# A hybrid RWKV-7 and neighbourhood-attention layer: low halves of four w_out weights made by ACT and adding DMAs, the first sums into x ahead of a small transpose, and two steps of the load order moved

## The chip, the cores and the metric

One core of one Trainium2 chip runs the kernel. The core has five instruction engines, each with an order of its own: TensorE (PE), VectorE (DVE), ScalarE (ACT), GpSimd (POOL) and SyncE (SP), which here only issues DMAs. POOL issues some DMAs too. The metric is the device time of one execution in microseconds (us).

## What is computed

One layer over 640 tokens: 512 noisy latent tokens on a grid 64 wide and 128 context tokens. The layer, shortened from the reference (the shifts sh, scales sc and gates g come from a conditioning vector; the recurrent and the attention branch are two functions of their own, not shown):

```python
sh1, sc1, g1, sh2, sc2, g2 = _modulation(cvec, p["w_ada"], p["b_ada"])
h = _rmsnorm(x, p["norm1_g"]) * (1.0 + sc1) + sh1
u_rw, u_na, gate_rw, gate_na = jnp.split(h @ p["w_in"], IN_SPLITS, axis=-1)
o_rw, s_new = _rwkv_branch(u_rw, s0, ...)                 # 512 wide
o_na = _na_latent(q, k, v, ctx_k, ctx_v, p["na_rpb"])     # 512 wide
merged = (jax.nn.sigmoid(gate_rw) * (o_rw @ p["w_o_rwkv"])
          + jax.nn.sigmoid(gate_na) * (o_na @ p["w_o_na"]))   # 1024 wide
x = x + g1 * (merged @ p["w_out"])                        # w_out: 1024 x 1024
h2 = _rmsnorm(x, p["norm2_g"]) * (1.0 + sc2) + sh2
x = x + g2 * ((jax.nn.silu(h2 @ p["ffn_w1"]) * (h2 @ p["ffn_w3"])) @ p["ffn_w2"])
```

All of it is float32 in and out.

## The kernel before, in words

Each matmul is made of three on fp32r operands: high half of the weight by high and by low half of the activation, and low half of the weight by high half of the activation. A weight tile of 128x1024 (512 KB) goes through three steps. `wdma` (L156 to L168) has SP load it into a staging tile `wst`. `wcast` (from L179) makes the high half `whi` with a rounding copy on ACT (L185) and the low half `wlo`, as a rule by a subtraction on DVE (L188, `wst` less `whi`). With `eng=pool` the low half comes another way: ACT writes the rounded weight negated into `wlo` (L183) and a DMA issued by POOL adds `wst` onto it (L184). `wload` does both steps.

In the middle part, `stream` (from L788) runs a fixed list of weight units one after the other and feeds their matmuls in between other work. It keeps the staging loads of two units ahead queued on SP, and queues them at the start of a unit. The units a0 to a3 and b0 to b3 are the merge: they multiply w_o by the attention and recurrent outputs `o`, seven tiles that come back from memory (`o_d`) by `o_load` (L1473): tiles 0 to 3 for the a units, 4 and 5, and 6 when it is there, for the b units. The second part is loaded before unit a0 runs. What the units add up is kept in `mt` and other tiles of 128x640. The eighth tile of the outputs, `o3`, never leaves the core and is merged last.

The last merge, `last_gen` (L1638 to L1656), runs 16 halves of 320 tokens, two for each of eight feature tiles. For a half PE runs 3 matmuls (L1649) into one of three PSUM buffers `fl`; DVE multiplies by the gate's tile `pre` or `tr` (L1650), which frees that buffer, and adds what the units left in `mt` (L1652); ACT makes the high half of m (L1653) and POOL the low half (L1654). From the sixth half on, PE puts two matmuls of w_out's first half (L303) behind each half; PE's order is written out there by hand, the other engines' order comes from a scheduler.

w_out's first half (`w0`) takes four weights, w_out[0] to w_out[3], as chunks of two feature tiles each; 30 matmuls a chunk, 120 in all, into accumulators `acc` for five blocks of 128 tokens. Chunks 0 to 2 run over all blocks, and the last (chunk 3) block by block, so that block 0 is ready first. w_out[0] is cast before the merge. Then `x` (L1678) and the gate rows `G` (L1683) are loaded; 16 small PE transposes (L1709) bring shift and scale rows into `pc`, from which DVE makes s and m (L1711 to L1713); and `add_gated` (L1685 to L1689) does for each block `tt = acc * G` (L1688), which frees the accumulator, and `x = x + tt` (L1689). The second half, with w_out[4] to w_out[7], follows, and behind it the feed-forward part (L1810 and on, with L1854 for its low halves) to the end.

Staging tiles and high and low halves come from pools: two staging tiles and two pairs of halves in the pool of the outer part (w_out[0], [4], [6]), two of each in a pool for w_out[1] to [3], and one staging tile and two pairs in a pool that opens when that one closes (w_out[5], [7]).

Of the kernel before, what the change touches and what calls it, by code (L numbers as in the profile page):

```python
# [107 lines left out]
def body(ctx: ExitStack, tc: tile.TileContext, xs, xp, cols, consts, w_ada, b_row, w_rw, w_qkv,  # L108
# [26 lines left out]
    def nm(s):  # L135
        cn[0] += 1
        return f"{s}_{cn[0]}"
# [59 lines left out]
    def wload(src, eng=None):  # L197
        return wcast(wdma(src), eng)
# [81 lines left out]
    def tok_gen(pss, pp, lhs_hl, chunks, kts, toks, tag="acc", bufs=5, tail=1, keep=None):  # L280
# [7 lines left out]
        for ci, src in enumerate(chunks):  # L288
            ws.append(src if isinstance(src, (tuple, list)) else wload(src))
# [494 lines left out]
    def stream(order):  # L784
# [10 lines left out]
        for i, g in enumerate(order):  # L795
            while len(ds) < min(i + 3, len(us)):
                ds.append(us[len(ds)][1]())
# [5 lines left out]
            for j in range(n):  # L803
                if j == n // 8:
                    later(lambda i=i: cast(i + 1), (1.05, 0), -off[0])
                next(it)
                tick(1)
                if j == n - 1:
                    drain(it)
                    done.add(g)  # L810
                    if i + 1 < len(order) and order[i + 1] == "a0":
                        o_load(4, 6)
                        if "O2" in marks:
                            o_load(6, 7)
                yield True
# [261 lines left out]
    with ExitStack() as s3:  # L1077
# [394 lines left out]

        def o_load(a, b):  # L1473
# [3 lines left out]
            for q in range(a, b):  # L1477
# [100 lines left out]
        with tc.manual_schedule(engines=FIRST):  # L1578
# [54 lines left out]
            c0 = wload(w_out[0])  # L1633
# [30 lines left out]
    w0 = w_out_gen(pss, [c0] + [w_out[q] for q in range(1, 4)], range(5))  # L1664
# [39 lines left out]
    pc = pp.tile([P, 512], F32, tag="tp", name=nm("pc"))  # L1704
    for j in range(2):
        arow = sb.tile([P, 1024], F32, tag="xn", bufs=3, name=nm("arow"))[0:2, :]
        sp.dma_start(arow, adr[:, (6 + 2 * j) * 512:(8 + 2 * j) * 512])
        for kt in range(8):
            pe.transpose(pc[:, 16 * j + 2 * kt:16 * j + 2 * kt + 2], arow[:, kt * 128:(kt + 1) * 128],  # L1709
                         K[0:2, KO["ident"]:KO["ident"] + 2])  # L1710
    dve.tensor_copy(s2, V(pc[:, :], [[2, 8], [1, 2]]))  # L1711
    dve.tensor_scalar(out=m2, in0=V(pc[:, :], [[2, 8], [1, 2]], 16), scalar1=1.0, scalar2=None, op0=ALU.add)
    dve.tensor_tensor(out=m2, in0=m2, in1=V(C[:, :], [[1, 8], [0, 2]], CO["n2"]), op=ALU.mult)  # L1713
    for i in range(5):
        add_gated(pss[i], i, 0, 0.5)
# [375 lines left out]
```

## Time and profile before

| what | us |
|---|---|
| median of 3 runs (lowest, highest) | 1175.58 (1175.09, 1177.53) |
| the profiled execution, its own time | 1175.43 |
| its span in the trace | 1173.7 |
| PE busy in the span | 1125.1 |
| DVE busy | 778.6 |
| ACT busy | 531.9 |
| POOL busy | 193.2 |

The mean granted clock of PE in the profiled execution was 0.991 of full speed. All times below are in us from the start of the span. A row of a timeline gives start, duration, engine, line, operation, result<-operands, shapes and the number of instructions in the group, and in brackets the idle time ahead of it with what ended that. Rows named SPq or POOLq are issues of DMAs. A wait view gives, for an engine, the total, the number and the longest of its waits by line and by what it waited for. The whole span has three stretches for what follows: the middle part to 662, the last merge with w_out's first half from 662 to 704, and the second half and the feed-forward part after that.

### The profile page before, as it was taken

What the parts mean: (1) busy time and instruction counts of PE and PEld (TensorE: products, weight loads), DVE (VectorE), ACT (ScalarE), POOL (GpSimd) and SP (SyncE); (2) the same over time, 40 slices, a digit from 0 to 9 for tenths busy, and PEclk for the clock granted to TensorE, in tenths of its full rate; (3) what the DMA queues carried; (4) which work ended last, traced back from release to release, by engine and by line L of the source; (5) the groups of instructions that cost most, each with busy time, mean ns of one, the idle gap of its engine ahead of it and who ended that gap; (6) DMA issues with size and microseconds to landing.
All of it is one profiled execution on the core that took longest, in us unless ns stands there. A gap on an engine that the chain in (4) does not pass through costs nothing.

```text
span 1173.7 us, 26876 instructions
## 1 busy us (share of the span) xinstructions
PE 1125.1 (96%) x11160; PEld 995.6 (85%) x11160; DVE 778.6 (66%) x1643; ACT 531.9 (45%) x1050; POOL 193.2 (16%) x260
## 2 busy tenths in 40 slices
PE   6999999999999999999899899999999999999998
PEld 4688877789888988888788777899899989998997
DVE  4565465559558747935576847887577756875775
ACT  4444666554564665556443324654224423441330
POOL 1162244320101202111100231100000000001000
PEclk9999999999999999999899999999999999999999
DMA  9752767554433523433843641312312222232122
GB/s 338 265 115 83 240 227 231 188 162 103 105 84 93 139 69 91 111 99 93 281 122 114 216 159 55 108 58 88 108 54 91 91 89 65 80 108 90 54 81 99
DMA packets 60194, 148.11 MB, mean 126 GB/s; under 512 B 7428, under 2 KB 22404, under 8 KB 60072
## 3 DMA queue, kind: packets, MB, share of 16 engines
q1 hardware_dynamic: 55464, 131.56, 34.3%
q0 software_dynamic: 3744, 13.63, 6.0%
q8 instruction: 88, 1.44, 0.5%
q10 hardware_dynamic: 864, 1.20, 0.4%
q14 instruction: 34, 0.28, 0.1%
HBM read 118.41 MB, written 14.32 MB: 113 GB/s over the span
## 4 chain that ended last, share of the span: by engine, by line
PE 60%; DVE 10%; ACT 3%; issue 2%; DMA 2%; SPq 0%; POOL 0%; DVEq 0%; ACTq 0%; POOLq 0%
PE f L1810 21%; PE acc L303 16%; PE fl L216 11%; PE w L1367 1%; PE w L1394 1%; DVE pr L1293 1%; PE w L1407 1%; PE mm L216 1%; PE w L1379 1%; PE w L1191 1%; DVE RL L1297 1%; DVE Rt L1327 1%; PE w L1424 1%; PE w L1385 1%; PE w L1239 1%
## 5 line engine op out<-in xcount | busy, mean ns | idle before, releaser
L1810 PE MATMUL f<-t,whi 128*128 128x320 f32 x640 | 142.4, 311 | 0.0
L1810 PE MATMUL f<-b,whi 128*128 128x320 f32 x608 | 135.6, 310 | 2.1 <-ACT b L204 1.8
L303 PE MATMUL acc<-whi,u 128*128 128x512 f32 (+1 forms) x448 | 136.0, 385 | 0.0
L216 PE MATMUL fl<-h,whi 128*128 128x320 f32 x672 | 121.2, 320 | 1.0 <-issue 1.0
L1810 PEld LDWEIGHTS f<-t,whi 128*128 128x128 f32 x640 | 108.1, 189 | 0.0
L185 ACT CAST whi<-wst 128x1024 fp32r<-128x1024 f32 (+1 forms) x77 | 79.1, 1033 | 62.3 <-PE acc L303 42.7
L216 PEld LDWEIGHTS fl<-h,whi 128*128 128x128 f32 x672 | 101.3, 188 | 5.8 <-issue 1.2
L1810 PEld LDWEIGHTS f<-b,whi 128*128 128x128 f32 x608 | 102.0, 188 | 3.3 <-ACT b L204 2.2
L1810 PE MATMUL f<-t,wlo 128*128 128x320 f32 x320 | 99.4, 310 | 0.0
L303 PEld LDWEIGHTS acc<-whi,u 128*128 128x128 f32 x448 | 83.5, 188 | 16.7
L1810 PE MATMUL f<-b,wlo 128*128 128x320 f32 x304 | 94.3, 310 | 2.2 <-DVE wlo L1854 2.2
L1851 ACT CAST whi<-ws 128x1024 fp32r<-128x1024 f32 x40 | 42.0, 1051 | 109.0 <-PE f L1810 44.4
L188 DVE TENSOR_TENSOR wlo<-wst,whi 128x1024 fp32r<-128x1024 f32 (+2 forms) x59 | 63.4, 1086 | 36.9 <-ACT whi L185 36.3
L303 PE MATMUL acc<-wlo,u 128*128 128x512 f32 (+1 forms) x224 | 86.3, 385 | 0.0
L1865 POOL TENSOR_TENSOR ws<-wst 128x512 f32<-128x512 f32 x20 | 28.0, 1402 | 340.8 <-DVE wlo L1854 226.7
L303 PE MATMUL acc<-whi,h 128*128 128x512 f32 x240 | 78.0, 399 | 0.9 <-DVE h L428 0.9
L216 PE MATMUL fl<-h,wlo 128*128 128x320 f32 x336 | 63.3, 321 | 0.0
L1688 DVE SCALAR_TENSOR_TENSOR tt<-acc,G 128x512 f32<-128x512 f32 (+1 forms) x51 | 34.5, 680 | 42.7 <-PE acc L303 42.7
L1851 ACT CAST whi<-wst 128x1024 fp32r<-128x1024 f32 (+1 forms) x48 | 41.3, 869 | 42.3 <-PE acc L303 25.1
L1810 PEld LDWEIGHTS f<-t,wlo 128*128 128x128 f32 x320 | 60.5, 189 | 0.0
L1810 PEld LDWEIGHTS f<-b,wlo 128*128 128x128 f32 x304 | 57.2, 188 | 2.5 <-DVE wlo L1854 2.5
L1854 DVE TENSOR_TENSOR wlo<-ws,whi 128x1024 fp32r<-128x1024 f32 x40 | 54.7, 1366 | 6.6 <-ACT whi L1851 6.6
(342 smaller groups left out, 2507.8 us busy)
## 6 DMA issues: line engine op xcount, KB each, us to landing
wst<-in_w_dram SPq DMA_DIRECT2D x66, 512.0 KB
wst<-in_w_rw_dram SPq DMA_DIRECT2D x31, 512.0 KB
wlo<-wst POOLq DMA_DIRECT2D x26, 512.0 KB, 4.8
wa<-in_w_ada_dram SPq DMA_DIRECT2D x24, 512.0 KB
f<-in_w_ada_dram SPq DMA_DIRECT2D x16, 512.0 KB
wst<-in_w_qkv_dram SPq DMA_DIRECT2D x12, 512.0 KB
o<-o_d SPq DMA_DIRECT2D x14, 320.0 KB
x<-in_xs_dram SPq DMA_DIRECT2D x8, 512.0 KB
```

Source lines behind the costliest of these rows:

```text
L185: act.copy(hi[:, :n], st[:, :n])
L188: dve.tensor_tensor(out=lo[:, a:b], in0=st[:, a:b], in1=hi[:, a:b].bitcast(F32), op=ALU.subtract)
L216: pe.matmul(ps[:, :t1 - t0], w[:, a:a + 128], x[:, k0 + kt, t0:t1], start=n == 0, stop=n == 3 * nk - 1)
L303: pe.matmul(pss[i][:, a:b], lhs(x, kt, ts_), w[:, cs_], start=ki == 0 and n == 0, stop=ki == last and n == 2)
L1191: pe.matmul(pr[h][hrows[h ^ i], o_], x[hrows[h], :], R_[hrows[h], l, :], start=True, stop=True)
L1239: pe.matmul(pt[h][hrows[h ^ i], o_], S.BK[l // 10][hrows[h], l % 10, i, :], idh(h), start=True, stop=True)
L1293: dve.tensor_tensor(out=prv, in0=V(RL[:, s + 1 + a, :], [[32, b - a], [0, s]], s), in1=V(RL[:, s, :], [[0, b - a], [1, s]]), op=ALU.mult)
L1688: dve.scalar_tensor_tensor(out=tt, in0=ps[:, a:b], scalar=c, in1=G[:, g, sl], op0=ALU.mult, op1=ALU.mult)
L1810: pe.matmul(ps[:, :H2], w_[:, c_], x_[:, kt, :], start=first and kt + n == 0, stop=last and kt == 3 and n == 2, skip_group_check=more)
L1851: act.copy(r[0][:, :width], src())
L1854: dve.tensor_tensor(out=r[1][:, :width], in0=src(), in1=r[0][:, :width].bitcast(F32), op=ALU.subtract)
L1865: eng_x(PRM["se"][i - 1]).tensor_tensor(out=o_, in0=x, in1=y, op=op)
```

## The change

There are four edits. First, `stream` queues the staging loads of the unit after next in the middle of a unit (a quarter in for some sizes) and no longer at its start. Second, `o_load(4, 6)` is called when a0 has run, not before it; `got` keeps a tile from being loaded twice. Third, w_out[0] to w_out[3] get `eng=pool`. Fourth, the sums into x come ahead of the transposes in the program, in a region in which DVE keeps the order in which the code is written.

```diff
--- before.py
+++ after.py
@@ -277,7 +277,7 @@
             pass
         return pss
 
-    def tok_gen(pss, pp, lhs_hl, chunks, kts, toks, tag="acc", bufs=5, tail=1, keep=None):
+    def tok_gen(pss, pp, lhs_hl, chunks, kts, toks, tag="acc", bufs=5, tail=1, keep=None, eng=None):
 
 
         pss.update((i, pp.tile([P, 512], F32, tag="tp" if i == 5 else tag, bufs=3 if i == 5 else bufs,
@@ -286,7 +286,7 @@
         last = len(kts) - 1
         ws, n0 = [] if keep is None else keep, len(chunks) - tail
         for ci, src in enumerate(chunks):
-            ws.append(src if isinstance(src, (tuple, list)) else wload(src))
+            ws.append(src if isinstance(src, (tuple, list)) else wload(src, eng))
             ks = [2 * ci + k for k in range(2)]
 
             if ci >= n0:
@@ -793,8 +793,6 @@
         ds.append(us[1][1]())
         yield True
         for i, g in enumerate(order):
-            while len(ds) < min(i + 3, len(us)):
-                ds.append(us[len(ds)][1]())
             while wait.get(g) not in marks:
                 yield False
             n, f = us[i][0], us[i][3]
@@ -803,12 +801,14 @@
             for j in range(n):
                 if j == n // 8:
                     later(lambda i=i: cast(i + 1), (1.05, 0), -off[0])
+                if j == (n // 2 if n == 48 else n // 4) and i + 2 < len(us):
+                    ds.append(us[i + 2][1]())
                 next(it)
                 tick(1)
                 if j == n - 1:
                     drain(it)
                     done.add(g)
-                    if i + 1 < len(order) and order[i + 1] == "a0":
+                    if g == "a0":
                         o_load(4, 6)
                         if "O2" in marks:
                             o_load(6, 7)
@@ -1470,11 +1470,14 @@
                 marks.add("O2")
 
 
+        got = set()
+
         def o_load(a, b):
 
             if not o:
                 o.extend(Two([]) for _ in range(2))
-            for q in range(a, b):
+            for q in sorted(set(range(a, b)) - got):
+                got.add(q)
                 for i, (t, t_d) in enumerate(zip(o, o_d)):
                     if len(t.ts) == q // 4:
                         t.ts.append(hp_t("o", i, q // 4))
@@ -1630,7 +1633,7 @@
                 S = S2
             weave(og)
             need(*(f"b{i}" for i in range(4)))
-            c0 = wload(w_out[0])
+            c0 = wload(w_out[0], pool)
 
 
     pp = open_pool(ctx, "pp4", bufs=3, space=PSUM)
@@ -1661,7 +1664,7 @@
     pss = {}
     trp = open_pool(hs, "trp")
     weights(hs, 2, 2)
-    w0 = w_out_gen(pss, [c0] + [w_out[q] for q in range(1, 4)], range(5))
+    w0 = w_out_gen(pss, [c0] + [w_out[q] for q in range(1, 4)], range(5), eng=pool)
     with tc.manual_schedule(engines=MANUAL):
         for h, _ in enumerate(last_gen()):
             for _ in range(PRM["lw"][h]):
@@ -1701,18 +1704,19 @@
                       name=f"b{x[0]}{x[1]}{i}") for i in range(2)] for x in halves2}
     sb = open_pool(ctx, "p4")
     load_gate(4)
-    pc = pp.tile([P, 512], F32, tag="tp", name=nm("pc"))
-    for j in range(2):
-        arow = sb.tile([P, 1024], F32, tag="xn", bufs=3, name=nm("arow"))[0:2, :]
-        sp.dma_start(arow, adr[:, (6 + 2 * j) * 512:(8 + 2 * j) * 512])
-        for kt in range(8):
-            pe.transpose(pc[:, 16 * j + 2 * kt:16 * j + 2 * kt + 2], arow[:, kt * 128:(kt + 1) * 128],
-                         K[0:2, KO["ident"]:KO["ident"] + 2])
-    dve.tensor_copy(s2, V(pc[:, :], [[2, 8], [1, 2]]))
-    dve.tensor_scalar(out=m2, in0=V(pc[:, :], [[2, 8], [1, 2]], 16), scalar1=1.0, scalar2=None, op0=ALU.add)
-    dve.tensor_tensor(out=m2, in0=m2, in1=V(C[:, :], [[1, 8], [0, 2]], CO["n2"]), op=ALU.mult)
-    for i in range(5):
-        add_gated(pss[i], i, 0, 0.5)
+    with tc.manual_schedule(engines={mybir.EngineType.DVE}):
+        for i in range(5):
+            add_gated(pss[i], i, 0, 0.5)
+        pc = pp.tile([P, 512], F32, tag="tp", name=nm("pc"))
+        for j in range(2):
+            arow = sb.tile([P, 1024], F32, tag="xn", bufs=3, name=nm("arow"))[0:2, :]
+            sp.dma_start(arow, adr[:, (6 + 2 * j) * 512:(8 + 2 * j) * 512])
+            for kt in range(8):
+                pe.transpose(pc[:, 16 * j + 2 * kt:16 * j + 2 * kt + 2], arow[:, kt * 128:(kt + 1) * 128],
+                             K[0:2, KO["ident"]:KO["ident"] + 2])
+        dve.tensor_copy(s2, V(pc[:, :], [[2, 8], [1, 2]]))
+        dve.tensor_scalar(out=m2, in0=V(pc[:, :], [[2, 8], [1, 2]], 16), scalar1=1.0, scalar2=None, op0=ALU.add)
+        dve.tensor_tensor(out=m2, in0=m2, in1=V(C[:, :], [[1, 8], [0, 2]], CO["n2"]), op=ALU.mult)
 
 
     nr = [{} for _ in range(5)]
```

The changed file has three more lines ahead of the last merge, so L1650 before is L1653 behind, and L1688 is L1691.

Where the third edit shows on DVE, the rows at the start of the last merge are as follows, before and behind. wlo_9058 is the low half of w_out[0], wlo_9457 and wlo_9464 are that of w_out[4], the rows of L1525 and L1528 belong to the last unit b3, and pre is the gate of the first feature tile.

```order
L1525 SCALAR_TENSOR_TENSOR mx_9017<-mx_9017,fl_9041 128x320
L1527 TENSOR_TENSOR bv_8415<-bv_8415,mx_9017 128x320
L188 TENSOR_TENSOR wlo_9058<-wst_9055,whi_9057 128x1024
L188 TENSOR_TENSOR wlo_9457<-wst_9454,whi_9456 128x1024
L1650 SCALAR_TENSOR_TENSOR pre_9079<-pre_9079,fl_9095 128x320
L1650 SCALAR_TENSOR_TENSOR pre_9079<-pre_9079,fl_9103 128x320
```

```order
L1528 SCALAR_TENSOR_TENSOR mx_9017<-mx_9017,fl_9041 128x320
L1530 TENSOR_TENSOR bv_8415<-bv_8415,mx_9017 128x320
L188 TENSOR_TENSOR wlo_9464<-wst_9461,whi_9463 128x1024
L1653 SCALAR_TENSOR_TENSOR pre_9080<-pre_9080,fl_9096 128x320
L1653 SCALAR_TENSOR_TENSOR pre_9080<-pre_9080,fl_9104 128x320
```

One of the two subtractions ahead of the first L1650 is gone; those of w_out[1], [2] and [3] are gone from their places further on in the same way.

What takes their place on POOL stands among the m's of the merge. wlo_9058, wlo_9262, wlo_9299 and wlo_9336 are the low halves of w_out[0] to [3]; before, the rows of L184 are absent and those of the m's are the same.

```order
L184 DMA wlo_9058<-wst_9055 128x1024
L1657 TENSOR_TENSOR m_9070<-pre_9080,m_9068 128x320 x2
L1657 TENSOR_TENSOR m_9070<-pre_9082,m_9068 128x320 x2
L1657 TENSOR_TENSOR m_9070<-pre_9084,m_9068 128x320 x2
L184 DMA wlo_9262<-wst_9259 128x1024
L1657 TENSOR_TENSOR m_9070<-pre_9086,m_9068 128x320
L184 DMA wlo_9299<-wst_9296 128x1024
L1657 TENSOR_TENSOR m_9070<-pre_9086,m_9068 128x320
...
L1657 TENSOR_TENSOR m_9071<-tr_9094,m_9069 128x320 x2
L184 DMA wlo_9336<-wst_9333 128x1024
```

On ACT each of the four gets a pass of L183. The casts of w_out[1] and [2], which stood behind the third and the sixth m, now stand with these passes behind the sixth and the seventh. On SP, four later loads now wait for an adding DMA whose memory they take over: w_out[6] for that of w_out[0], w_out[3] for that of w_out[1], w_out[5] for that of w_out[2], and G for that of w_out[3].

Where the fourth edit shows on DVE, at the end of w_out's first half, the rows before and behind are these. wlo_9333 is the low half of w_out[3], wlo_9481 and wlo_9488 are that of w_out[5], pc is the result of the small transposes.

```order
L188 TENSOR_TENSOR wlo_9333<-wst_9330,whi_9332 128x1024
L1711 COPY s_9381<-pc_9410 128x16
L1712 TENSOR_SCALAR m_9380<-pc_9410 128x16
L1713 TENSOR_TENSOR m_9380<-m_9380,C 128x16
L1688 SCALAR_TENSOR_TENSOR tt_9434<-acc_9143,G 128x512
L1688 SCALAR_TENSOR_TENSOR tt_9437<-acc_9144,G 128x512
L1689 TENSOR_TENSOR x_0_9374<-x_0_9374,tt_9434 128x512
```

```order
L1691 SCALAR_TENSOR_TENSOR tt_9416<-acc_9144,G 128x512
L1692 TENSOR_TENSOR x_0_9378<-x_0_9378,tt_9416 128x512
L1691 SCALAR_TENSOR_TENSOR tt_9419<-acc_9145,G 128x512
...
L188 TENSOR_TENSOR wlo_9488<-wst_9485,whi_9487 128x1024
L1692 TENSOR_TENSOR x_3_9381<-x_3_9381,tt_9425 128x512
...
L1717 COPY s_9385<-pc_9431 128x16
```

The three operations on pc now stand behind the fifth sum, and the low halves of w_out[5] and [6] among the sums. On PE eleven of the sixteen transposes moved from the end of chunk 3 to a place ahead of its first matmul with w_out[3]'s low half; five stayed. The first two edits move SP rows alone: one staging load of the early part behind another load, one behind two, and one write of tna_d ahead of two of o's loads.

## The prediction

> **What bounds the kernel now.** I read first the chain of work that ended last, by engine. The reader is to see that TensorE (PE) alone carries most of it, so an edit is worth the idle time that it takes from PE.
>
> ```profile
> PE 60%; DVE 10%; ACT 3%; issue 2%; DMA 2%; SPq 0%; POOL 0%; DVEq 0%; ACTq 0%; POOLq 0%
> ```
>
> Second, the waits of PE, by line and by what it waited for (total us, times, longest).
>
> ```profile
> PE fl L216 <- DMA o<-o_d: 3.1, 7, 1.0
> ...
> PE fl L1649 <- DVE pre L1650: 2.5, 1, 2.5
> ...
> PE acc L303 <- DVE tt L1688: 1.9, 2, 1.2
> ...
> PE fl L1649 <- DVE tr L1650: 1.2, 2, 0.7
> ```
>
> Three of the four lie where the change works: L1649 is the last merge, L1688 the sums into x. Third, PE's timeline there, with the idle time before a group in brackets.
>
> ```profile
> 665.78 1.71 PE L1649 MATMUL fl<-o,f 128*128 128x320 f32 x9 [2.46 <-DVE pre L1650]
> ...
> 669.81 0.63 PE L303 MATMUL acc<-wlo,m 128*128 128x512 f32 x1
> ...
> 674.89 0.70 PE L1649 MATMUL fl<-o,f 128*128 128x320 f32 x3 [0.52 <-DVE tr L1650]
> ...
> 677.79 0.70 PE L1649 MATMUL fl<-o,f 128*128 128x320 f32 x3 [0.65 <-DVE tr L1650]
> ...
> 703.08 1.15 PE L1709 MATMUL pc<-K,arow 2*128 2x2 f32 x16
> ...
> 705.38 0.72 PE L303 MATMUL acc<-whi,m 128*128 128x512 f32 x2 [1.16 <-DVE tt L1688]
> ...
> 707.78 0.73 PE L303 MATMUL acc<-whi,m 128*128 128x512 f32 x2 [0.73 <-DVE tt L1688]
> ```
>
> Fourth, the windows of those stretches (length; busy PE, PE's weight loads, DVE, ACT, POOL; granted clock, DMA share, GB/s).
>
> ```profile
> 663.70:667.10 3.40, 1.32 (x9) 1.32 (x9) 3.40 (x7) 0.14 (x1) 0.00 (x0) 1.00 0.67 223
> 667.10:670.50 3.40, 3.25 (x9) 2.18 (x9) 3.40 (x6) 2.13 (x4) 2.77 (x3) 0.50 0.48 154
> 670.50:674.00 3.50, 3.50 (x21) 3.13 (x20) 3.50 (x7) 2.22 (x4) 2.81 (x2) 1.00 0.00 0
> 674.00:678.00 4.00, 2.83 (x13) 1.68 (x12) 4.00 (x7) 0.92 (x2) 4.00 (x4) 1.00 0.41 133
> 680.50:703.10 22.60, 22.60 (x101) 18.42 (x99) 6.46 (x9) 3.78 (x8) 6.79 (x7) 1.00 0.49 177
> ```
>
> From 663.7 to 678 DVE is busy all the time and PE is not: the last merge is bound by DVE. From 680.5 PE is busy throughout, 100 matmuls of w_out in 22.60, 0.226 each.
>
> **The change, part by part.** The profiled execution took 1175.43 us, 0.15 under the median 1175.58, and the sum is made against it.
>
> Term 1: low halves off DVE. DVE's own rows:
>
> ```profile
> 662.98 2.35 DVE L188 TENSOR_TENSOR wlo<-wst,whi 128x1024 fp32r<-128x1024 f32 x2
> ...
> 672.14 1.21 DVE L188 TENSOR_TENSOR wlo<-wst,whi 128x1024 fp32r<-128x1024 f32 x1
> ...
> 675.83 1.50 DVE L188 TENSOR_TENSOR wlo<-wst,whi 128x1024 fp32r<-128x1024 f32 x1
> ```
>
> The two at 662.98 are those of w_out[0] and w_out[4]; only the first goes, half of 2.35 = 1.17, and PE's wait of 2.46 for L1650 behind them shrinks to 1.29. The 1.21 and 1.50 (w_out[1], w_out[2]) stand right ahead of the L1650 that end PE's waits of 0.52 and 0.65; both waits go, and what is late next is PE's own work between. The sum is 1.17 + 0.52 + 0.65 = **2.3**. The most it can be is all the DVE time, 1.17 + 1.21 + 1.50 = 3.9, if DVE alone sets the pace; the least, if the two short waits come back behind L1652, is 1.2. I take 2.3, since each of its parts is a wait that a row shows. The fourth (w_out[3], after the merge) stands on no wait.
>
> What replaces them: four passes of ACT (L183) and four POOL issues with an adding DMA (L184).
>
> ```profile
> L183 ACT ACTIVATE wlo<-wst 128x1024 fp32r<-128x1024 f32 x26 | 27.3, 1051 | 0.0
> ...
> L184 POOL DMA_DIRECT2D wlo<-wst x26 | 23.3, 895 | 176.3 <-ACT wlo L183 174.6 <-issue 0.5 <-ACT U L532 0.5
> ```
>
> ACT gets 1.05 four times. Between 670.5 and 678 it was busy 2.22 + 0.92 of 7.5 us, so two of them fit without PE seeing them. POOL gets 0.9 four times, one after the sixth m and one after the seventh. There POOL has no room (4.00 of 4.00), so the eighth m comes up to 1.8 later, at about 678.7, and the second chunk of w_out wants it about 2 us after its own start at 680.4. That hides it. Five m's are done by 674 in these windows, the sixth takes about 1 us more, and the merge is then 1.2 earlier and less in DVE's way: w_out[1]'s issue comes at about 673.5, w_out[2]'s, one m and one issue later, near 675.5.
>
> The DMAs themselves are the open price. This is the median landing over the program, a long case in the chain, and the longest (read with 2.87 MB of other traffic beside it):
>
> ```profile
> wlo<-wst POOLq DMA_DIRECT2D x26, 512.0 KB, 4.8
> ```
>
> ```profile
> 586.72 6.65 DMA wlo<-wst
> ```
>
> ```profile
> wlo<-wst POOLq DMA_DIRECT2D x1, 512.0 KB, 10.0
> ```
>
> Deadlines against these. w_out[0]: ACT is free for it where the cast stands now,
>
> ```profile
> 659.36 1.04 ACT L185 CAST whi<-wst 128x1024 fp32r<-128x1024 f32 x1
> ...
> 689.40 1.05 ACT L185 CAST whi<-wst 128x1024 fp32r<-128x1024 f32 x1 [3.18 <-PE acc L303]
> ```
>
> so it is issued at 660.4 and lands at 665.2, or 667.0 at 6.65; the first matmul with the low half (669.81, less 1.17) wants it at 668.6. It fits up to 8.2 us. The chunks behind the merge take 30 x 0.226 = 6.8 each and start, back from 703.1, at 696.3, 689.5 and 682.7, all 2.3 earlier then, and the low half enters two matmuls (0.45) after a start. w_out[1]: from 673.5 to 678.3, wanted at 680.8, fits up to 7.3. w_out[2]: wanted at 687.6, fits. w_out[3]: its staging buffer is cast when PE frees the tile, at 689.40 now, 687.1 then; the cast and the pass take 2.1, the issue is at 689.2, the landing at 694.0. The third matmul of chunk 3 wants it at 696.3 - 2.3 + 0.45 = 694.45, and eleven of the sixteen small transposes, now ahead of it, put that off by 11/16 of 1.15 = 0.8, to 695.2. It fits up to 6.0: at 6.65 PE stalls 0.65, at 10.0 it stalls 4.0. I take 4.8 and no stall, since most of the 26 are near it and since G, the next transfer, now waits for this landing and cannot run beside it. The window before w_out[0]'s DMA lands is the crowded one:
>
> ```profile
> 660.00:663.40 3.40, 2.90 (x18) 2.64 (x18) 3.07 (x7) 1.45 (x2) 0.00 (x0) 1.00 0.98 375
> ```
>
> DVE is busy 3.07 of 3.40 there and nearly without pause after. The nearest row to a POOL-issued DMA under a busy DVE is
>
> ```profile
> 580.00:600.00 20.00, 19.79 (x302) 19.02 (x301) 19.44 (x83) 9.53 (x19) 3.51 (x4) 1.00 0.63 178
> ```
>
> with DVE busy 19.44 of 20 us, in which the landing of 6.65 lies. The Trainium skill ("SBUF — State Buffer", section "SBUF: two separate sides") states that a two-port DVE operation locks GpSimd out, so that a DMA issued there waits for its descriptors until DVE lets go. By that rule strictly each add here would wait out a DVE instruction of about 1 us; by the row it lands within 6.65 all the same, so the sum by the one is the sum by the other unless several such waits add up, and that case is the slower rival below.
>
> Term 2: sums first. Now DVE's queue holds the copies of pc ahead of the sums:
>
> ```profile
> 704.26 0.17 DVE L1711 COPY s<-pc 128x16 f32<-128x16 f32 x1 [12.55 <-PE pc L1709]
> 704.64 1.28 DVE L1688 SCALAR_TENSOR_TENSOR tt<-acc,G 128x512 f32<-128x512 f32 x2
> ```
>
> DVE stands idle 12.55 for transposes that PE runs at the end of chunk 3, and the first sum starts only at 704.64, though block 0, first of five in chunk 3, is done near 698. PE wants freed accumulators at 704.2 and again at 707: 1.16 + 0.73 = **1.9**. With the sums first, the first starts when its block is done and G is there. G is issued and landed now by:
>
> ```profile
> 691.74 0.80 SPq L1683 DMA_DIRECT2D G<-adr  x2
> ```
>
> ```profile
> 698.00:700.00 2.00, 2.00 (x10) 1.69 (x9) 0.00 (x0) 0.00 (x0) 0.00 (x0) 1.00 0.01 4
> ```
>
> so about 6 us after its issue. Behind w_out[3]'s landing it is issued at 694 and there by 697.5 to 699.5; four sums and their additions at 0.64 each take 5.1, but the first accumulator is free 0.64 after G, by 700.2, well ahead of PE, which comes to the second half at 703.08 + 1.15 - 2.3 = 701.9. Both waits go (bounds 0 and 1.9). Behind DVE's waiting sums now stand the low halves of w_out[5], [6], [7]; w_out[5]'s staging load waits for w_out[2]'s add and lands near 700.5, its low half is made by 703.5 and wanted at 706.
>
> Parts 1 and 2: on SP alone a 512 KB load moves behind one or two other loads near 128 and 189 us, and one write of tna_d ahead of two of o's loads. Their issue times:
>
> ```profile
> 128.43 0.37 SPq L167 DMA_DIRECT2D wst<-in_w_rw_dram  x1
> ```
>
> ```profile
> 564.67 2.55 SPq L1481 DMA_DIRECT2D o<-o_d  x4
> 567.88 0.32 SPq L588 DMA_DIRECT2D tna_d<-fl  x1
> ```
>
> One place in the queue is worth 0.3 to 0.4; what is loaded is used by units much later (o's second part from about 604). I take 0, bounds -0.5 and +0.5 (a wait of PE there is 1.0 at most, row of o above).
>
> Sum: 1175.4 - 2.3 - 1.9 = **1171.2**. After 708 nothing is moved, PE and DVE follow one another, and the gain is carried to the end.
>
> **The rivals.**
>
> The clock falls differently. PE runs at half clock from 667.10 (0.50 above) and again after this window:
>
> ```profile
> 769.50:772.90 3.40, 1.20 (x8) 1.10 (x8) 3.37 (x5) 1.38 (x2) 0.00 (x0) 1.00 0.10 13
> 772.90:776.30 3.40, 3.40 (x15) 3.40 (x14) 2.12 (x4) 2.01 (x4) 1.28 (x1) 0.50 0.38 141
> ```
>
> ```profile
> 738.55 0.42 PE L1810 MATMUL f<-b,whi 128*128 128x320 f32 x1 [1.76 <-ACT b L204]
> ...
> 771.81 0.41 PE L1810 MATMUL f<-b,wlo 128*128 128x320 f32 x1 [2.20 <-DVE wlo L1854]
> ```
>
> Each slow stretch costs half of 3.4 = 1.7 where PE sets the pace. The gaps ahead were 2.46 and 2.20, the one of 1.76 was let pass. The gap of 2.46 shrinks to 1.29, so the first slow stretch may go; DVE sets the pace there, so I count nothing for it beyond the bound of 3.9. The second gap stays but moves by 4.2 us, 0.8 past one period of 3.4: it may split between two periods (1169.5), or another gap may start falling whole into one (1172.9). The Trainium skill ("TensorE: Matmul & The Clock Gate", section "What's actually happening") says the rate is halved after an idle window of about 3.4 us, on a window that runs freely. By that rule neither gap would trigger, and nothing would be lost or won; the rows, busy 1.32 and 1.20 of 3.40 and halved all the same, say otherwise. Chance 0.14.
>
> The low half of w_out[0] is late: at 10.0 us it lands at 670.4, 1.8 after it is wanted. For it: DMA share 0.98 at its issue; against: the share falls to 0.67 right after. Term 1 falls to 0.5, **1173.0**. Chance 0.08.
>
> Term 2 is eaten: w_out[3]'s landing and G behind it slip together, DVE waits and PE with it; a slip of 1.2 + 1.9 = 3.1 us takes it whole. For it: G queues behind a landing; against: the median again. **1173.1**. Chance 0.10.
>
> Slower: adding DMAs land slowly under a busy DVE each time. At x us each, PE loses x - 7.3 for w_out[1] (which covers w_out[0]) and x - 6.0 for w_out[3]. From x = 8.8 this is over 4.2 and the change loses. At the 10.0 of the row, 2.7 + 4.0 = 6.7, less 4.2 is 2.5, and a gap of 4.0 brings a slow stretch of 1.7: 1175.4 + 2.5 + 1.7 = **1179.6**. Against: the median of 4.8. Chance 0.10.
>
> It doesn't do what it says: DVE fills the gaps with L1652 and PE's next work is late anyway, term 1 and 2 both give under 0.5: **1175.4**. Chance 0.06.
>
> **How the numbers follow.** The forecast has 0.52. About 0.2%, 2.35 us, is what a measurement of this kernel tells from no change, so faster means under 1173.2 and slower over 1177.9. Faster: 0.50 of the forecast, 0.13 of the clock case, 0.05 each of the two late cases, 0.73. Slower: 0.09 of its rival. Same: the rest, 0.18. The range goes down to 1168.8 (term 1 at 3.9, or the slow stretch gone) and up to 1175.0 (both late cases); left out are the slower rival, most of the last case and 0.04 below.
>
> **What would show it.** Right: PE's wait at L1649 near 1.3 and no second and third one, half clock gone near 667 or not, w_out[0] to [3] landing within 6 us, the first sum near 698 to 700 and no wait of PE for L1688. Wrong: PE waiting for wlo at L303, POOL's m in PE's waits, G landing after 701, or the gap near 770 with another clock.

## The result and the profile after

The changed kernel took 1170.43 us (median of 6 runs, 1168.79 to 1171.30), the kernel before beside it 1175.74 (6 runs, 1175.09 to 1178.13). The ratio is 0.9946, with a 95% interval of 0.9935 to 0.9957: faster by 0.54%. A second measurement beside other runs gave 0.9950 (0.9931 to 0.9969). The profiled execution took 1170.39 us with a span of 1168.6.

PE's waits after, by line (L1652, L1653 and L1657 are L1649, L1650 and L1654 of before). The waits for the sums are no longer in the list, a small one for an adding DMA is new, and the one for POOL's m has grown from 0.15 to 0.44.

```profile
PE fl L1652 <- DVE pre L1653: 1.3, 1, 1.3
...
PE acc L303 <- POOL m L1657: 0.4, 1, 0.4
...
PE fl L1652 <- DVE tr L1653: 0.4, 1, 0.4
...
PE acc L303 <- DMA wlo<-wst: 0.2, 1, 0.2
```

PE's timeline after, in the last merge. The wait of 2.46 is now 1.33; the first matmul with w_out[0]'s low half waits 0.19 for its landing; of the two short waits for DVE one of 0.40 is left.

```profile
663.71 1.59 PE L1652 MATMUL fl<-o,f 128*128 128x320 f32 x9 [1.33 <-DVE pre L1653]
...
667.48 0.50 PE L303 MATMUL acc<-wlo,m 128*128 128x512 f32 x1 [0.19 <-DMA wlo<-wst]
...
673.19 0.71 PE L1652 MATMUL fl<-o,f 128*128 128x320 f32 x3 [0.40 <-DVE tr L1653]
```

The windows after (columns as in the windows before). DVE is still busy all the time from 662.7 to 677.4, POOL now too from 670.5, and PE is at full clock (1.00) throughout; from 677.4 PE does not wait.

```profile
662.70:667.00 4.30, 2.74 (x14) 2.12 (x14) 4.30 (x10) 1.18 (x3) 1.56 (x2) 1.00 0.77 185
667.00:670.50 3.50, 3.31 (x19) 2.64 (x18) 3.50 (x9) 2.05 (x5) 2.58 (x4) 1.00 0.58 166
670.50:674.00 3.50, 3.10 (x18) 2.46 (x17) 3.50 (x7) 3.50 (x6) 3.50 (x5) 1.00 0.42 152
674.00:677.40 3.40, 3.31 (x18) 2.67 (x17) 3.40 (x5) 1.45 (x5) 3.40 (x6) 1.00 1.04 205
677.40:699.00 21.60, 21.60 (x104) 17.73 (x103) 7.49 (x12) 4.25 (x7) 6.80 (x8) 1.00 0.80 257
699.00:704.00 5.00, 5.00 (x26) 3.94 (x25) 4.75 (x8) 2.00 (x2) 0.00 (x0) 1.00 0.09 14
```

DVE's timeline after, at the sums and, earlier, at one addition of the merge. The first sum starts at 696.68, when G lands, and not at 704.64; the addition at 675.61 took 3.10 us, of which more below.

```profile
675.61 3.10 DVE L1655 TENSOR_TENSOR tr<-P,tr 128x320 f32<-128x320 f32 x1
...
696.68 0.69 DVE L1691 SCALAR_TENSOR_TENSOR tt<-acc,G 128x512 f32<-128x512 f32 x1 [14.00 <-DMA G<-adr]
```

To see where time went, the starts of three matmuls are compared in every profile, the 8271st, 8342nd and 8471st in PE's order (before: at 661.6, 680.5 and 709.7). "Merge" is the time between the first two, "next" between the other two.

| kernel | merge | next | start to merge | ratio of time to before |
|---|---|---|---|---|
| before | 18.97 | 29.21 | 661.56 | 1 |
| changed | 16.40 | 27.25 | 660.62 | 0.9946 |
| changed, again | 16.42 | 27.26 | 659.62 | 0.9950 |
| e_loads (edits 1, 2) | 19.42 | 29.78 | 660.71 | 0.9981 |
| o_only (edit 2) | 18.98 | 29.23 | 660.20 | 0.9991 |
| stage_only (edit 1) | 18.97 | 29.21 | 662.12 | 0.9990 |
| e_adds (edit 3) | 16.39 | 29.59 | 660.12 | 0.9980 |
| e_sums (edit 4) | 18.98 | 26.94 | 661.54 | 0.9972 |
| e_adds_sums (edits 3, 4) | 18.58 | 27.25 | 661.95 | 0.9968 |
| f_c0only (w_out[0] of edit 3) | 19.66 | 29.22 | 660.46 | 1.0001 |
| f_w123 (the rest of edit 3) | 19.32 | 29.61 | 662.84 | 1.0003 |
| f_pcfirst | 16.40 | 29.86 | 658.70 | 0.9986 |
| g_w4 | 14.98 | 27.88 | 659.90 | 0.9939 |
| h_early | 14.42 | 29.49 | 659.74 | 0.9966 |

From the profile of before to that of the changed kernel the merge gave 18.97 - 16.40 = 2.57 and the stretch after it 29.21 - 27.25 = 1.96. The way to the merge gave 0.94 and the rest took 0.42 more, together the 5.1 between the spans. The way to the merge differs by 1.00 between the two profiles of the changed kernel too, with no edit between them.

One reading of the diff has to be put right. The eleven transposes that run ahead of chunk 3's first matmul with w_out[3]'s low half are moved by the third edit and not by the fourth: they run early in e_adds and f_w123, and in e_sums all sixteen stay together at the end of the chunk.

### The profile page after: what moved, and what is told of

It reads as the page before. It is cut to its first block, busy times and chain, and to the rows that moved or that the text cites. A ratio compares the mean times of both kernels' runs of the same rounds, so it can differ in the third digit from the quotient of the medians.

```text
span 1168.6 us, 26884 instructions
## 1 busy us (share of the span) xinstructions
PE 1123.1 (96%) x11160; PEld 995.0 (85%) x11160; DVE 775.6 (66%) x1639; ACT 535.4 (46%) x1054; POOL 194.3 (17%) x264
## 4 chain that ended last, share of the span: by engine, by line
PE 60%; DVE 7%; issue 7%; ACT 3%; DMA 1%; SPq 0%; POOL 0%; DVEq 0%; ACTq 0%; POOLq 0%
PE f L1814 23%; PE acc L303 16%; PE fl L216 10%; DVE pr L1293 1%; PE mm L216 1%; PE w L1394 1%; DVE RL L1297 1%; PE w L1367 1%; PE w L1191 1%; PE w L1407 1%; DMA o<-o_d 1%; PE w L1379 1%; PE w L1169 1%; ACT wlo L183 1%; PE w L1239 0%
## 5 line engine op out<-in xcount | busy, mean ns | idle before, releaser
L188 DVE TENSOR_TENSOR wlo<-wst,whi 128x1024 fp32r<-128x1024 f32 (+2 forms) x55 | 58.3, 1072 | 31.8 <-ACT whi L185 31.2
L1691 DVE SCALAR_TENSOR_TENSOR tt<-acc,G 128x512 f32<-128x512 f32 (+1 forms) x51 | 34.7, 680 | 59.3 <-PE acc L303 45.3
```

The lines of the kernel that those rows point to most:

```text
L188: dve.tensor_tensor(out=lo[:, a:b], in0=st[:, a:b], in1=hi[:, a:b].bitcast(F32), op=ALU.subtract)
L1691: dve.scalar_tensor_tensor(out=tt, in0=ps[:, a:b], scalar=c, in1=G[:, g, sl], op0=ALU.mult, op1=ALU.mult)
```

## The experiments

Intervals are 95%. Microseconds worked out from a ratio are taken on the 1176.8 that before took beside these runs. All times of single stretches are from one profile each.

### Edits alone

e_loads is the kernel before with the diff's first two edits, e_adds with the third, e_sums with the fourth, e_adds_sums with the third and fourth, as printed above.

> The kernel before with the first two edits alone (staging loads half a unit later, o's second part behind a0). The changed kernel was already 0.95 us ahead of the kernel before at the start of the last merge, which the prediction did not count. Theory A (these edits move nothing on PE; the 0.95 is where clock windows fell, in one profiled execution): no difference, 1175.7 within 0.5, and the shift of PE's matmuls against before at 661 us will be another number than -0.95. Theory B (the two edits take waits from PE before 660 us): about 0.9 faster, 1174.8, and PE's shift at 661 us again near -0.9.

Measured: 0.9981 (0.9972 to 0.9990), 2.2 us less (1.2 to 3.3). So theory A falls, and theory B's 0.9 lies below the interval. The start of the merge came at 660.71, 0.85 ahead of before, but the profiled execution took 1176.32, more than the median of its twelve (1174.68), and does not show the gain; its stretch after the merge (29.78) has a halved period of the clock from 705.23 in it. Where PE gained is taken up below.

> The kernel before with the third edit alone (w_out[0] to [3] by ACT and adding DMAs). Theory A (the terms are separate and add up): PE's matmuls gain 2.3 to 2.7 between 662 and 682 us, the wait of PE for L1688 stays near 1.9 in total, time 1173.0 to 1173.4. Theory C (the sums are what matters, and the merge's gain is handed back because G waits for w_out[3]'s landing and the sums come late): gain of 2.3 to 2.7 by 682 but the wait for L1688 grows beyond 1.9 by what was gained, time near 1175.

Measured: 0.9980 (0.9969 to 0.9992), 2.4 us less (0.9 to 3.6). The merge took 16.39, 2.58 less, and the wait for the sums stayed:

```profile
PE acc L303 <- DVE tt L1688: 2.0, 2, 1.2
```

The profile is as theory A has it, and C falls: G was issued later (692.19 and not 691.74, with the merge 2.58 shorter), but PE paid no more for the sums than before. The time is about 1 above theory A's 1173.0 to 1173.4 (median 1174.35). The profiled execution, with 1171.88, is the second fastest of twelve that reach up to 1177.45, so the profiles don't show whether most executions have a merge of 16.4.

> The kernel before with the fourth edit alone (sums into x ahead of the three operations on pc, DVE in written order). Theory A: the two waits of PE for L1688 (1.16 and 0.73) go and nothing else moves, 1.9 less, 1173.8. Theory D (part of what is gained comes from the third edit, since the subtraction for w_out[3] stands ahead of the sums on DVE and the next low halves behind them): one of the two waits stays, 0.7 to 1.2 less, near 1174.8.

Measured: 0.9972 (0.9959 to 0.9984), 3.3 us less (1.9 to 4.8). The stretch after the merge took 26.94, 2.27 less; no wait of PE for L1688 is left, and the merge keeps its two longest waits:

```profile
665.77 1.59 PE L1649 MATMUL fl<-o,f 128*128 128x320 f32 x9 [2.46 <-DVE pre L1650]
...
677.77 0.71 PE L1649 MATMUL fl<-o,f 128*128 128x320 f32 x3 [0.65 <-DVE tr L1650]
```

Theory A again; the fourth edit needs nothing of the third, nor the early transposes. The stretch is 0.31 shorter than the changed kernel's 27.25, though PE waits in neither: where the transposes run in two groups and not in one, PE's matmuls around them fall 0.3 behind, a price of the third edit that the sum did not have.

> The third and the fourth edit together, without the first two. Theory A: as the changed kernel, 1170.4 to 1171.4, PE's shift from 661 to 706 us near -4.4. Theory B (the first two edits are worth 0.9): 1171.3 or more, clearly above the changed kernel. If the sum of the gains of the third and of the fourth edit alone differs from the gain of both by over 0.7, the terms are not separate.

Measured: 0.9968 (0.9955 to 0.9981), 3.8 us less (2.2 to 5.3). The stretch after the merge took 27.25, as in the changed kernel, but the merge 18.58 and not 16.40. On DVE, POOL, ACT and PE the order of the merge is the same in both. PE and DVE there:

```profile
675.90 0.71 PE L1649 MATMUL fl<-o,f 128*128 128x320 f32 x3 [1.65 <-DVE tr L1650]
...
678.86 0.70 PE L1649 MATMUL fl<-o,f 128*128 128x320 f32 x3 [0.87 <-DVE tr L1650]
```

```profile
673.65 1.80 DVE L1652 TENSOR_TENSOR tr<-P,tr 128x320 f32<-128x320 f32 x1
675.37 0.87 DVE L1650 SCALAR_TENSOR_TENSOR tr<-tr,fl 128x320 f32<-128x320 f32 x2
676.16 2.24 DVE L1652 TENSOR_TENSOR tr<-P,tr 128x320 f32<-128x320 f32 x2
```

An addition that takes 0.48 alone took 1.80, while the multiplications between (0.87 for two) kept their time. Here the stretched additions end right ahead of the multiplications that PE waited 1.65 and 0.87 for. In the changed kernel the long addition (3.10, from 675.61) cost PE nothing: its last wait in the merge, of 0.40, ended at 673.19, ahead of it. Four profiles with the third edit (the changed kernel twice, e_adds, f_pcfirst) have the one pattern, with an addition of 3.10 or 3.11 and a merge of 16.4, and this one has the other; what decides between them stays open. The profiled execution here took 1173.36, the median of nine that lie between 1169.54 and 1174.83. The gains of the third and the fourth edit alone add up to 5.7, that of both is 3.8; the intervals overlap, so the times alone don't show whether this is more than scatter.

### The two halves of the third edit

f_c0only changes one line of before, f_w123 the others of the third edit:

```diff
-            c0 = wload(w_out[0])
+            c0 = wload(w_out[0], pool)
```

```diff
-    w0 = w_out_gen(pss, [c0] + [w_out[q] for q in range(1, 4)], range(5))
+    w0 = w_out_gen(pss, [c0] + [w_out[q] for q in range(1, 4)], range(5), eng=pool)
```

> The kernel before with w_out[0]'s low half alone by ACT and an adding DMA. Theory A (term 1 is made of three waits, each its own): PE's wait at the start of the merge falls from 2.46 to about 1.3, those of 0.52 and 0.65 stay, and the stretch from 661.6 to 680.5 (18.97 before, 16.40 with all four) takes about 17.8. Theory G (DVE is one long queue, and only its total counts): the same 17.8 here, but the wait that goes at the start shows up again later.

Measured: 1.0001 (0.9993 to 1.0010). The first wait fell to 1.33 as foretold, and then the merge took 19.66, longer than before:

```profile
663.55 1.59 PE L1649 MATMUL fl<-o,f 128*128 128x320 f32 x9 [1.33 <-DVE pre L1650]
...
675.57 0.70 PE L1649 MATMUL fl<-o,f 128*128 128x320 f32 x3 [2.80 <-DVE tr L1650]
```

```profile
672.15 1.90 DVE L188 TENSOR_TENSOR wlo<-wst,whi 128x1024 fp32r<-128x1024 f32 x1
673.98 1.14 DVE L1652 TENSOR_TENSOR tr<-P,tr 128x320 f32<-128x320 f32 x1
```

The subtraction that took 1.21 in before took 1.90, beside POOL, which was then subtracting without a pause. What was gained at the start came back, and more, as one wait of 2.80. Theory A's "others stay" falls; G's second half is what happened.

> The kernel before with the low halves of w_out[1] to [3] alone by ACT and adding DMAs. Theory A: the wait of 2.46 stays, those of 0.52 and 0.65 go, the merge takes about 17.8. Theory G (DVE's total counts): 18.97 less 1.21 and 1.50, 16.3. Theory H (POOL's issues and m's hold up DVE's additions, as where three of them took 1.80 and 2.24 us in one of the profiles): 18.5 or more.

Measured: 1.0003 (0.9991 to 1.0014). The wait of 2.46 stayed, one of 1.70 came, and the merge took 19.32: theory H.

```profile
680.47 0.71 PE L1649 MATMUL fl<-o,f 128*128 128x320 f32 x3 [1.70 <-DVE tr L1650]
```

```profile
676.97 3.05 DVE L1652 TENSOR_TENSOR tr<-P,tr 128x320 f32<-128x320 f32 x2
```

So neither half shortens the merge alone, and both together shorten it by 2.58 in e_adds's profile.

### The order on DVE at the sums

f_pcfirst is the changed kernel with the region's two blocks exchanged:

```diff
     with tc.manual_schedule(engines={mybir.EngineType.DVE}):
-        for i in range(5):
-            add_gated(pss[i], i, 0, 0.5)
         pc = pp.tile([P, 512], F32, tag="tp", name=nm("pc"))
...
         dve.tensor_tensor(out=m2, in0=m2, in1=V(C[:, :], [[1, 8], [0, 2]], CO["n2"]), op=ALU.mult)
+        for i in range(5):
+            add_gated(pss[i], i, 0, 0.5)
```

> The changed kernel with the three operations on pc put ahead of the five sums again, in written order on DVE; PE, ACT and POOL keep their orders, the small transposes of PE their new places. Theory A (the order on DVE is what term 2 is made of): PE's two waits for the sums come back, 1.9 in total, and the stretch from 680 to 710 us takes about 29.2 and not 27.25. Theory E (the place of the transposes on PE, eleven of them earlier, is what helps): the stretch stays near 27.3 and the time that of the changed kernel.

Measured: 0.9986 (0.9975 to 0.9997), against 0.9946 and 0.9950 of the changed kernel. The merge is again 16.40, the stretch after it 29.86, 2.61 longer than in the changed kernel, and the waits are back, in three pieces that add up to 1.93:

```profile
700.33 0.72 PE L303 MATMUL acc<-whi,m 128*128 128x512 f32 x2 [1.21 <-DVE tt L1691]
701.66 0.74 PE L303 MATMUL acc<-whi,m 128*128 128x512 f32 x2 [0.36 <-DVE tt L1691]
702.99 0.74 PE L303 MATMUL acc<-whi,m 128*128 128x512 f32 x2 [0.36 <-DVE tt L1691]
```

Theory A, and E falls: the transposes have the changed kernel's places here and the waits are back, and in e_sums they have the old places and the waits are gone. The other 0.68 of the 2.61 lies between the matmuls around the three stops. By the ratios f_pcfirst is 4.2 to 4.7 us behind the changed kernel, more than the stretch shows. Its profiled execution, 1171.39, is the fastest of eleven that reach up to 1178.60, so what the slower ones paid for stays open; a merge of the longer pattern, as in e_adds_sums, is one possibility, and no profile shows it.

### The first two edits apart

> The kernel before with the second edit alone (o's second part behind a0: on SP one write of tna_d goes ahead of two of o's loads). The four profiles with o's second part ahead of a0 took 12.72 to 13.16 us between PE's matmuls at 562 and 575 us, the two with it behind a0 11.80 and 11.96, and the clock was halved there for two periods in the former and for one in the latter. Theory B1 (the second edit does that): 11.8 to 12.0 in that stretch, one halved period, about 1.0 us faster, 1175.8 if before is 1176.8. Theory B2 (chance, by where the clock's periods fall): 12.7 to 13.2, or two halved periods, and no difference in time.

> The kernel before with the first edit alone (staging loads half a unit later). The first two edits together were 0.19% faster (0.10 to 0.28), more than the 1.0 us of the stretch at 562 to 575. Theory B3 (the first edit brings the rest, about 1 us, in the start or near 130 to 190 us, where SP's loads change places): about 1 us faster. Theory A (as predicted): within 0.5 of before; the rest is scatter of the measurement.

Measured: o_only 0.9991 (0.9982 to 1.0000), stage_only 0.9990 (0.9981 to 0.9999): each about 1 us less, hardly told from none. Between PE's matmuls at 562 and 575 o_only took 11.59 with one halved period of the clock, stage_only 12.83 with two, as theory B1 had it. Two later runs broke the rule: the changed kernel's second profile has the second edit and took 12.92 with two, f_w123 has it not and took 11.68 with one. What separates all fourteen profiles, found afterwards, is where the clock's period lies. The first halved period begins between 1.46 us before and 0.52 after the end of PE's last wait for o; in the seven with two it begins 0.62 or more before that end, in the seven with one 0.55 or less before it, or after. The windows of before and of o_only, period by period:

```profile
568.11:571.52 3.41, 2.36 (x10) 2.12 (x10) 0.00 (x0) 0.00 (x0) 0.00 (x0) 0.50 1.06 329
571.52:574.93 3.41, 3.41 (x47) 2.55 (x49) 2.62 (x8) 0.92 (x1) 0.00 (x0) 0.50 1.03 312
```

```profile
569.31:572.73 3.42, 3.26 (x12) 2.86 (x12) 0.66 (x2) 0.00 (x0) 0.00 (x0) 0.50 1.08 315
572.73:576.14 3.41, 3.19 (x142) 2.77 (x141) 3.05 (x15) 2.84 (x5) 0.00 (x0) 1.00 1.00 332
```

Here a halved period in which PE was busy 2.36 is followed by another and one with 3.26 is not, but this share does not decide it: in e_adds_sums 3.17 was followed by another, in h_early 2.85 was not.

```profile
568.65:572.06 3.41, 2.85 (x11) 2.81 (x12) 0.26 (x1) 0.00 (x0) 0.00 (x0) 0.50 1.07 327
```

With the second edit six of seven profiles have one period, without it one of seven. Further halved periods near 23, 234 and 343 us are in some profiles and not in others, and of the changed kernel's two profiles one has all three and the other none, so they come without an edit. Whether the second edit moves the period near 570 or the draw of the executions did stays open, and with it where e_loads' 2.2 us come from.

### The changed kernel again, and two further steps

> The changed kernel once more, beside the others. Theory A: 0.9946 of before within 0.001; the merge 16.4 and the stretch after it 27.25 again; one halved period near 569. Theory H (DVE's additions are held up by POOL at random): a merge of 18 or more in this profile.

Measured: 0.9950 (0.9931 to 0.9969), the merge 16.42, the next stretch 27.26, as theory A; but two halved periods near 567, where theory A had one.

g_w4 gives w_out[4] the same treatment:

```diff
-        beside(w_out_gen(pss, [w_out[4 + q] for q in range(4)], (0, 1, 2), tail=2, keep=w1s))
+        beside(w_out_gen(pss, [wload(w_out[4], pool)] + [w_out[5 + q] for q in range(3)], (0, 1, 2), tail=2, keep=w1s))
```

> The changed kernel with the low half of w_out[4] also by ACT and an adding DMA, so that no subtraction stands ahead of the last merge on DVE. Theory A (DVE's subtraction is the whole of PE's remaining wait of 1.33 at the start of the merge): that wait falls to 0.2 or less, the merge from 661.6 to 680.5 takes about 15.3 and not 16.4, 1.1 faster than the changed kernel. Theory F (adding DMAs crowd each other: w_out[0]'s landed 0.2 to 0.5 after PE wanted it as it is): PE waits for w_out[0]'s low half instead, 1 us or more, and the merge takes 16.4 or longer.

Measured: 0.9939 (0.9926 to 0.9951), the merge 14.98, 1.42 under the changed kernel. Both theories had a part: the wait for DVE fell to 0.19, and one of 1.28 for w_out[0]'s landing appeared, yet the merge gained more than the 1.1 of theory A. The next stretch gave 0.63 back, 0.32 of it as a wait for w_out[1]'s landing.

```profile
661.86 1.90 PE L1652 MATMUL fl<-o,f 128*128 128x320 f32 x9 [0.19 <-DVE pre L1653]
...
666.41 0.50 PE L303 MATMUL acc<-wlo,m 128*128 128x512 f32 x1 [1.28 <-DMA wlo<-wst]
```

h_early adds to g_w4 that w_out[0]'s L183 and its DMA come ahead of ACT's last two casts of o (`og_c0` passes the steps of `og` on and does this at the eighth):

```diff
+            def og_c0(gen):
+                for i, y in enumerate(gen):
+                    if i == 7:
+                        st, _, pl, nhl = wdma(w_out[0])
...
+                        act.activation(lo, st, AF.Copy, scale=-1.0)
+                        pool.dma_start(lo.bitcast(F32), st, accum_op=ALU.add)
...
-            weave(og)
+            weave(og_c0(og))
             need(*(f"b{i}" for i in range(4)))
-            c0 = wload(w_out[0], pool)
+            act.copy(c0[0], c0[2])
```

> The changed kernel with w_out[4]'s low half by an adding DMA too and w_out[0]'s pass of ACT and its adding DMA put ahead of ACT's last two casts of o, some 3.5 us earlier. Theory F2 (in the run with w_out[4] PE's wait of 1.28 for w_out[0]'s low half was only the late issue): that wait goes, the merge takes 13.8 to 14.2 and not 14.98, and the time is 0.9 under that run's 0.9939 of before. Theory I (the landing is set by the traffic on the DMA engines there, not by the issue): it lands no earlier than 665 and the wait stays over 0.8.

Measured: 0.9966 (0.9952 to 0.9980), not better than g_w4. The DMA was issued at 654.58 and landed at 659.21, 4.63 later, so theory I falls and the wait of 1.28 went, and the merge took 14.42, above theory F2's 13.8 to 14.2. PE waited for w_out[1]'s landing (678.73, in g_w4 677.83) instead, and the stretch after the merge took 29.49. The reason lies on SP: the load that waits for w_out[0]'s adding DMA now stood ahead of the rows tr and of two loads of w_out. These two were issued at 661.55 and 662.12, in g_w4 at 655.76 and 656.24, so ACT waited for one of them and w_out[1]'s adding DMA was issued 1.93 later than in g_w4:

```profile
659.27 0.33 SPq L167 DMA_DIRECT2D wst<-in_w_out_dram  x1
659.65 1.85 SPq L1660 DMA_DIRECT2D tr<-trw_d  x4
661.55 0.99 SPq L167 DMA_DIRECT2D wst<-in_w_out_dram  x2
...
672.36 1.06 ACT L183 ACTIVATE wlo<-wst 128x1024 fp32r<-128x1024 f32 x1 [2.01 <-DMA wst<-in_w_out_dram]
...
678.77 0.50 PE L303 MATMUL acc<-wlo,m 128*128 128x512 f32 x1 [1.92 <-DMA wlo<-wst]
```

Of all, g_w4 has the lowest ratio, though its interval overlaps that of the changed kernel.

## Why the prediction was right, point by point

- **Term 1, 2.3 us.** Measured 2.57 in the changed kernel's profile (2.58, 2.57 and 2.55 in three more, but 0.39 in e_adds_sums); the third edit alone is worth 2.4 in time (0.9 to 3.6). The size was right, its make-up was not, and that the sum came so near is in part luck. The sum 1.17 + 0.52 + 0.65 treated the waits as separate; f_c0only and f_w123 show that one part without the other shortens nothing, since DVE's additions and subtractions stretch beside POOL and the wait comes back elsewhere. The row of DVE busy for 3.50 of 3.50 and the bound of 3.9 were the better reading. By the durations of DVE's instructions, the subtractions ahead of and in the merge took 5.15 in before and 1.22 in the changed kernel, its sixteen additions 12.70 and 14.19, and its sixteen multiplications 7.6 both times: 3.93 left the queue, 1.49 came back beside POOL, and the difference of 2.44 is nearly the 2.57.
- **What hides POOL's issues.** "That hides it" was true of the matmuls that use the m's, and it missed that m's piled up behind two issues run without a pause, in which DVE's addition waits. In the changed kernel that cost PE nothing; in e_adds_sums, where additions of 1.80 and 1.84 fell right ahead of what PE wanted, the merge took 2.2 longer.
- **The adding DMAs.** w_out[0]'s took 7.7 us against the 4.8 that the sum used, and 8.2 was said to fit: PE, which came to it earlier than forecast, waited 0.19 (0.46 in e_adds, 0.49 in f_pcfirst). w_out[1]'s took 4.5, w_out[2]'s 6.8, w_out[3]'s 4.5, and G was there at 696.68 for the first sum. The rivals that rest on late landings did not come to pass, the first of them by a small margin.
- **Term 2, 1.9 us.** Measured 1.96, with the fourth edit alone 2.27, and f_pcfirst takes it all back. The mechanism was right. That the size is right too hides two small terms that nearly cancel: taking away the stops gains some 0.4 more than the waits of 1.89, and the transposes in two groups cost 0.3.
- **The first two edits at 0.** Together they measure 2.2 us (1.2 to 3.3), outside the bound of 0.5 given for them. This is the term of the sum that was wrong. The stretch near 570 accounts for about 1 us of it where it shows; the rest has no place in the profiles, in which the way to the merge scatters from 658.70 to 662.84. The gains of e_loads, e_adds and e_sums in time add up to 7.9, while the changed kernel has 5.3 and, measured again, 5.9. So the forecast of 4.2, with a term left out, came nearer than its parts would have it; with intervals of 1 to 1.5 to each side this may be scatter.
- **The clock.** The half clock near 667 went with the shorter gap, in all eight profiles with a gap of 1.33 or less; of the six with 2.46, five have it. The sixth, e_loads, has a merge of 19.42 without it, no shorter than before's, which fits that DVE sets the pace there. The gap near 770 no longer halved the clock, and the one before 738, which the prediction had "let pass" at 1.76, did (from 733.33). So of the first rival's two cases both came to pass, at two places, and cancelled; that they did is luck. Of the fourteen profiles thirteen have a halved period at one of the two places and none at both.
- **The signs.** Of those for "right" the wait near 1.3 and the end of PE's waits for L1688 came; a short wait for DVE was left, two of the four landings took over 6 us, and the first sum came at 696.68, earlier than 698. Of those for "wrong" three came, all small or cancelled: PE waiting for wlo (0.19), POOL's m in PE's waits (0.44, before 0.15) and the gap near 770 with another clock. As signs they were too coarse: each says that a wait or a landing is there, not how long it may be.

```profile
672.34 0.87 POOL L184 DMA_DIRECT2D wlo<-wst  x1
672.95 1.18 POOL L1657 TENSOR_TENSOR m<-pre,m 128x320 fp32r<-128x320 f32 x1
673.78 1.19 POOL L184 DMA_DIRECT2D wlo<-wst  x1
674.46 1.42 POOL L1657 TENSOR_TENSOR m<-pre,m 128x320 fp32r<-128x320 f32 x1
675.59 2.77 POOL L1657 TENSOR_TENSOR m<-tr,m 128x320 fp32r<-128x320 f32 x3
```

These rows of POOL in the changed kernel belong to the second point: the last three subtractions start at 675.59 and end at 678.36, and DVE's addition, started at 675.61, ends at 678.71, after the last of them.

## What to carry to other kernels

Read how long an engine's queue is without a pause before adding up the single waits that it causes: where it is always busy, only what leaves the queue counts, and what another engine takes on in its place can slow what stays. Three small operations that wait for something late, at the head of an in-order queue, cost the whole wait of what stands behind them; put what is ready first. A step that is moved earlier moves what waits for it in another queue too, and whatever stands behind that: in h_early one load came ahead of six others and held them up.

## What the runs showed of the hardware

- A DVE addition of two operands in SBUF (0.48 alone) that began with a run of three POOL subtractions ended only after the last of them: 3.10 us. By the profile, whose spans on POOL are rough, each of the three starts some 0.28 before the one ahead of it ends. Beside the run of five that follows, which overlap by 0.04, additions took 0.65 to 1.16 and ended within the run. Multiplications with one operand in PSUM took at most 0.48, sixteen of them in each of the fourteen profiles.

```profile
679.84 0.67 DVE L1655 TENSOR_TENSOR tr<-kk,tr 128x320 f32<-128x320 f32 x1
680.43 1.16 DVE L1655 TENSOR_TENSOR tr<-bv,tr 128x320 f32<-128x320 f32 x1
...
679.29 4.96 POOL L1657 TENSOR_TENSOR m<-tr,m 128x320 fp32r<-128x320 f32 x5 [0.93 <-ACT m L1656]
```

  The Trainium skill ("SBUF — State Buffer", section "SBUF: two separate sides") says that a DVE operation with two inputs in SBUF and a GpSimd operation that reads SBUF exclude each other for a whole instruction. The trace agrees on which operations suffer; it differs in that DVE once waited out three instructions of POOL, not one.
- POOL's adding DMAs of 512 KB landed 4.5 us after their issue with DVE busy throughout (w_out[1], 672.34 to 676.80) and 4.5 with DVE idle (w_out[3], 688.20 to 692.71), and 7.7 where other loads were on the way (w_out[0]). Over these three flights the DMA engines moved 140, 197 and 253 GB/s; w_out[2]'s 6.8 had 230, and in h_early one of 10.56 had 278. So the time follows the traffic, and a busy DVE alone did not make one late.
- In the fourteen profiles, from 15 to 1160 us, the clock was halved after periods of 3.41 us in which PE was busy 0.96 to 2.27, so a window need not be idle. Every full period under 1.5 was followed by a halved one, and of those between 1.5 and 2.3 some were and some were not (1.52 in after_again, from 478.2, was let pass). Whether a second halved period follows is not told by PE's share of the first: 3.17 was followed by one in e_adds_sums, 2.85 was not in h_early. The Trainium skill ("TensorE: Matmul & The Clock Gate", section "What's actually happening") speaks of an idle window; here a window half busy was enough, and the measurement decides.
